# A modulation gate's matrix-vector product: column tiles of the tensor engine, or sums on the vector engine between z's projections

## The chip, the core and the metric

The kernel runs on one core of one Trainium2 chip. The core has a tensor engine (PE) with its weight loads (PEld), a vector engine (DVE), a scalar engine (ACT), a GpSimd engine (POOL), and a sync engine (SP), which here issues nearly all DMA loads from one in-order queue. The metric is the device time of one execution in microseconds (us). Runs of this kernel differ by about 0.3%.

## What is computed

One decoder layer over 512 tokens of width 1024, in fp32. The input is normalised and modulated by a vector `c`; it is projected to the queries, keys and values of two head groups and to two gates `z_a`, `z_b`; group A does sliding-window attention with sinks, group B sparse attention with three branches (compressed, selected, window); each group's output is multiplied by SiLU(z); a last projection is scaled by the modulation's `gate` and added to the input.

```python
def hybrid_layer(x, c, w_ada, b_ada, ...):
    mod = jax.nn.silu(c) @ w_ada + b_ada
    shift, scale, gate = jnp.split(mod, 3, axis=-1)
    h = rms_norm(x, norm_gain) * (1 + scale[:, None, :]) + shift[:, None, :]
    proj = h @ w_in
    (q_a, k_a, v_a, z_a, q_b, kc, vc, ks, vs, kw, vw, z_b, g_b) = jnp.split(proj, ...)
    ...
    y = jnp.concatenate([o_a * jax.nn.silu(z_a), o_b * jax.nn.silu(z_b)], axis=-1)
    return x + gate[:, None, :] * (y @ w_out)
```

The case is about `gate` alone: 1024 values, each a sum over 1024 rows of the last third of `w_ada`, weighted by silu(c). `sc_col` holds silu(c) as 8 columns of 128 (one for each block of 128 rows), and `scz` the same columns padded to 32 wide with zeros for use as weights of a narrow matmul.

## The kernel before

The work runs in stages. The first (to about 57 us) computes shift and scale, normalises, and projects group A's q, k and v. The second (to about 164 us) projects group B's keys and values and its queries while group A's attention runs. The third (to about 270 us) projects z while group B's attention runs. The last is the output projection.

Attention runs in *slots* (one head of each of two groups of keys, one block of 128 queries). `run()` takes a slot through four steps: scores on PE; the row maximum on DVE, the exponential on ACT and the scaling by the reciprocal sum on DVE; transposes on PE, which ACT copies; and the product with the values on PE. Four slots are in different steps at a time. Between the steps `stream.adv(...)` draws work from a generator: `gen1()` in stage two, `gen2()` in stage three. `gen2()` runs the eight units of z's projection, `unit_col(...)`, eight blocks each; in each block are three matmuls of 128x512. fp32 weights are used as a high and a low part: `split()` (lines 171 and 172) makes `wh` on ACT and `wl` on DVE out of a raw tile. `with_posts()` runs one step of the first generator in the list `posts` with each block of a unit; `post_z` (SiLU) is put at the front of that list after each unit.

Raw weights come in 512 KB halves through `load_next()`, which issues the next of a fixed list (`raw_order`: ..., z_a0, gate0, z_a1, gate1, z_b0, gate2, z_b1, gate3, o0 to o3) on SP. It is called when a raw tile has had its last use; the new tile takes a free buffer of the pool, and its load waits for whatever last used that buffer. Since SP works in order, a load that waits holds those behind it.

The gate is made in four slices of 256 columns. `gate_slice(q)` multiplies with 8 calls of 128x32 by 128x256 (16 matmuls, since an fp32 matmul takes two) into four column tiles of one PSUM bank, and ACT copies the bank to `gacc`. The partition sums of `gacc` follow much later, with the first unit of the output projection (`pg`). `run()` calls a slice after the values' products of each of the first four of group B's eight groups of slots. Lines after the changed function stand 3 to 6 higher in the numbering of the changed kernel (scores L878 become L884, transposes L926/L936 become L932/L942, value products L953/L959 become L959/L965, gate sums L1033 become L1036).

Of the kernel before, what the change touches and what calls it, by code (L numbers as in the profile page):

```python
# [13 lines left out]
AF = mybir.ActivationFunctionType  # L14
OP = mybir.AluOpType
# [66 lines left out]
def hybrid_layer_kernel(ctx, tc, A, out):  # L82
    nc = tc.nc
    PE, DVE, ACT, POOL, SP = nc.tensor, nc.vector, nc.scalar, nc.gpsimd, nc.sync
# [9 lines left out]
    def T2(dt, name):  # L94
        return t2.tile([128, S], dt, name=name, tag="t2")
# [31 lines left out]
    gacc = con.tile([128, D], F32, name="gacc")  # L127
# [3 lines left out]
    sc_col = con.tile([128, 8], F32, name="sc_col")  # L131
# [13 lines left out]
    raws, pieces, pending = {}, {}, list(raw_order)  # L145

    def load_next():
        if pending:
            g, h = pending.pop(0)
            n = A["w_" + g].shape[3]  # L150
            t = rawp.tile([128, 4, GW], F32, name="raw")
            SP.dma_start(t[:, :, 0:n], A["w_" + g][h])
            raws[g, h] = t[:, :, 0:n]
# [53 lines left out]
    scz = con.tile([128, 8, 32], F32, name="scz")  # L207
# [92 lines left out]
    with in_order(tc) as begun:  # L300
# [29 lines left out]
        for k in range(8):  # L330
# [7 lines left out]
            if k % 4 == 3:  # L338
# [3 lines left out]
                for tb in range(NB):  # L342
                    PE.matmul(pr[:, tb:tb + 1], sacc[:, tb * 128:(tb + 1) * 128], ones, start=k == 3 and tb == 0,
                              stop=k == 7 and tb == NB - 1, skip_group_check=True)
# [113 lines left out]
    def W2(name, shape=(128, 512)):  # L458
        return mp.tile(list(shape), F32, name=name, tag="w2", bufs=5)
# [6 lines left out]
    def PJ():  # L466
        n_pj[0] += 1
        return (ps_px if n_pj[0] % 3 == 0 else ps_pj).tile([128, 512], F32, name="pj")
# [14 lines left out]
    def unit_col(g, ch, bank, src=(hh, hl)):  # L483

        for k in range(8):
            split_to(g, 2 * ch + k // 4, AHEAD)
            wh, wl = (x[:, k % 4, :] for x in pieces[g, 2 * ch + k // 4])
            for m, (w, h) in enumerate(((wh, src[0][k]), (wh, src[1][k]), (wl, src[0][k]))):
                PE.matmul(bank, w, h, start=k == 0 and m == 0, stop=k == 7 and m == 2)  # L489
            yield 0.65  # L490
# [3 lines left out]
    @contextmanager  # L494
    def block():

        with in_order(tc, chain, PE.engine) as last:
            yield
        chain.update(last)
# [209 lines left out]

    def gate_slice(q):  # L710

        pm = PJ()[:, 0:256]
        for h in range(2):
            for c in range(4):
                PE.matmul(pm[32 * c:32 * c + 32, :], scz[:, 4 * h + c, :], raws[f"gate{q}", h][:, c], start=h == 0,  # L715
                          stop=h == 1, skip_group_check=True)
            load_next()
        ACT.activation(gacc[:, 256 * q:256 * q + 256], pm, AF.Copy)

    posts = []  # L720

    def with_posts(gen):

        for cost in gen:
            if posts:
                c = next(posts[0], None)
                if c is None:
                    posts.pop(0)
                else:
                    cost += c  # L730
            yield cost

    def flush_posts():
        while posts:
            yield from posts.pop(0)
# [62 lines left out]
    def post_z(n, b):  # L798
        t = W2("zth")
        ACT.activation(t, b, AF.Tanh, scale=0.5)  # L800
        z = W2("sza") if n < 4 else T2(F32, "szb")
        DVE.scalar_tensor_tensor(z, t, 1.0, b, op0=OP.add, op1=OP.mult)
        yield 0.0
        if n < 4:
            make_y(n, o_a[n], z)
        else:
            sz[n - 4] = z
# [3 lines left out]
    def make_y(c, o, z):  # L811

        yf = W2("yf")
        DVE.scalar_tensor_tensor(yf, o, 0.5, z, op0=OP.mult, op1=OP.mult)
        yh[c], yl[c] = T2(F32R, f"yh{c}"), T2(F32R, f"yl{c}")
        ACT.activation(yh[c], yf, AF.Copy)
        DVE.tensor_tensor(yl[c], yf, yh[c].bitcast(F32), op=OP.subtract)

    def gen2():
        posts.append(cmp_attn())  # L820
        for n in range(8):
            b = PJ()
            yield from with_posts(unit_col(f"z_{'ab'[n // 4]}{n % 4 // 2}", n % 2, b))
            posts.insert(0, post_z(n, b))
        yield from flush_posts()


# [9 lines left out]
    def load_bias_b(r):  # L837
        for g in range(2):
            t = mp.tile([128, 512], F32, name="bias", bufs=4)
            src = line_d[1, 4 * g + r:4 * g + r + 1, :]  # L840
            SP.dma_start(t, bass.AP(tensor=src.tensor, offset=src.offset, ap=[[1, 128], [1, 512]]))
            bias["b", r, g] = t
# [51 lines left out]
    def slot_scale(sl):  # L894
        kind, r, br, i = sl["id"]
        P, dn, w = sl["P"], sl["dn"], sl["w"]
        gates = grev.rearrange("p i (g r c) -> p i g r c", g=2, c=3)[:, i, :, r]
        if br == 3:
            rr = sm.tile([128, 2, 2], F32, name="rr2", bufs=2)
            DVE.reciprocal(rr, dn)  # L900
            for g in range(2):
                for b in range(2):
                    v = P[:, g, 128 * b:128 * b + 128]
                    DVE.tensor_scalar(v, v, rr[:, g, b:b + 1], gates[:, g, 1 + b:2 + b], op0=OP.mult, op1=OP.mult)
            return
        rr = sm.tile([128, 2], F32, name="rr", bufs=4)
        DVE.reciprocal(rr, dn)
        for g in range(2):
            v = P[:, g, 0:w]
            if kind == "b":  # L910
                DVE.tensor_scalar(v, v, rr[:, g:g + 1], gates[:, g, br:br + 1], op0=OP.mult, op1=OP.mult)  # L911
            elif g:
                ACT.activation(v, v, AF.Copy, scale=rr[:, g:g + 1])
            else:
                DVE.tensor_scalar(v, v, rr[:, g:g + 1], None, op0=OP.mult)

    def slot_trans(sl):
        kind, r, br, i = sl["id"]
        P, w = sl["P"], sl["w"]
        nb = w // 128  # L920
        if nb <= 2:
            T = T2(F32, "ptT").rearrange("p (g b q) -> p g b q", g=2, b=2)
            pt = PT()
            for g in range(2):
                for b in range(nb):
                    PE.transpose(pt[:, (nb * g + b) * 128:(nb * g + b + 1) * 128], P[:, g, b * 128:(b + 1) * 128], ident)  # L926
            ACT.copy(T[:, :, 0:nb, :], rev(pt[:, 0:2 * nb * 128].rearrange("p (g b q) -> p g b q", g=2, b=nb)))  # L927
            sl["T"] = [T[:, g] for g in range(2)]
        else:
            sl["T"] = []  # L930
            for g in range(2):
                T = T2(F32, "ptT").rearrange("p (b q) -> p b q", b=4)  # L932
                sl["T"].append(T)
                pt = PT()
                for b in range(nb):
                    PE.transpose(pt[:, b * 128:(b + 1) * 128], P[:, g, b * 128:(b + 1) * 128], ident)  # L936
                ACT.copy(T[:, 0:nb, :], rev(pt[:, 0:nb * 128].rearrange("p (b q) -> p b q", b=nb)))
# [29 lines left out]
                o_a["b", r] = T2(F32, f"ob{r}")  # L967
                ACT.activation(o_a["b", r], o, AF.Copy)

    def run(slots, stream, more):  # L970

        n = len(slots)
        group = []
        for t in range(n + 3):
            per = PER_A if t < 16 else PER_B[t - 16 >= PER_B[2]]
            if t < n:
                kind, r, br, i = slots[t]["id"]
                if kind == "a" and i == 0 and r >= 2:
                    load_bias_b(r - 2)
            if 0 <= t - 2 < n:  # L980
                with block():
                    slot_trans(slots[t - 2])
            if 0 <= t - 1 < n:
                slot_scale(slots[t - 1])
            if t < n:
                with block():
                    slot_scores(slots[t])
            stream.adv(per / 2)
            if 0 <= t - 3 < n:
                group.append(slots[t - 3])  # L990
                kind, r, br, i = slots[t - 3]["id"]
                if i == NB - 1:
                    with block():
                        for sl in group:
                            slot_pv(sl)
                        if more and kind == "b":
                            more.pop(0)()
                    group = []
                    if kind == "b" and br == 2 and r + 2 < 4:
                        load_bias_b(r + 2)  # L1000
            stream.adv(per / 2)
# [7 lines left out]
    stream = Stream(gen12())  # L1009
# [3 lines left out]
    for r in range(3, 0, -1):  # L1013
        posts.insert(0, prep_q_a(r))
    run([{"id": ("a", r, 0, i)} for r in range(4) for i in range(NB)]
        + [{"id": ("b", r, *bi)} for r in range(4) for bi in [(3, 0)] + [(br, i) for br in (1, 2) for i in range(1, NB)]],
        stream, [lambda q=q: gate_slice(q) for q in range(4)])
    stream.drain()
    for r in range(4):
        if 4 + r not in yh:  # L1020
# [3 lines left out]
    gate = con.tile([128, 8], F32, name="gate")  # L1024
    pg = PJ()

    for n in range(8):
        xr = mp.tile([128, S], F32, name="xr", tag="qc", bufs=2)
        ACT.dma_start(xr, A["xT"][n])
        b = PJ()  # L1030
# [5 lines left out]
        f = W2("fin")  # L1036
# [72 lines left out]
```

## Time and profile before

| | us |
|---|---|
| median of three runs | 331.12 (330.75 to 331.83) |
| the profiled execution | 331.1 |
| its span, first to last instruction | 328.9 |
| PE busy | 320.3 |
| weight loads busy | 262.9 |
| DVE busy | 225.5 |
| ACT busy | 197.8 |

In the rows of a profile the first number is the start (timeline, chain) or the share; `x16` counts instructions; what stands in brackets or behind the last bar is the idle time of that engine just ahead, with what ended it. Tile names go without their buffer numbers.

### The profile page before, as it was taken

The numbers are of one execution on the slowest core, as the hardware profiler recorded it, in microseconds if no ns is written. First come the engines' busy times: TensorE is split into PE (matmuls) and PEld (weight loads), VectorE is DVE, ScalarE is ACT, GpSimd is POOL, SyncE is SP. The second block draws the span as 40 slices with busy tenths as digits, with TensorE's granted clock in tenths as the row PEclk, the third lists the DMA queues.
The fourth block names the chain that finished last, engine by engine and source line by source line (L and its number), as shares of the span: only waits on it lengthen the run. The fifth ranks groups of instructions, "written<-read, shape, count | busy, mean of one in ns | idle before, by whom it ended". The sixth has DMA issues, their size and how long they took to land.

```text
span 328.9 us, 6232 instructions
## 1 busy us (share of the span) xinstructions
PE 320.3 (97%) x2304; PEld 262.9 (80%) x2304; DVE 225.5 (69%) x661; ACT 197.8 (60%) x478; POOL 4.6 (1%) x22
## 2 busy tenths in 40 slices
PE   8999999999999899999999999999999999999995
PEld 3577888879999779999977778678788788788884
DVE  3557697999896248787899799686576784543320
ACT  5674645656887355994967758878487586421200
POOL 1000000000000000000000000000000000000000
PEclk9999999999999999999999999999999999999999
DMA  7999966600050883122042260535240022152321
GB/s 222 388 408 410 397 222 182 247 0 3 3 159 0 276 282 117 32 65 67 32 129 81 78 229 3 190 123 200 66 128 2 0 67 64 34 161 69 123 64 64
DMA packets 31062, 44.27 MB, mean 135 GB/s; under 512 B 1767, under 2 KB 23399, under 8 KB 31033
## 3 DMA queue, kind: packets, MB, share of 16 engines
q1 hardware_dynamic: 29880, 41.79, 37.4%
q10 hardware_dynamic: 1152, 2.10, 2.2%
q8 instruction: 18, 0.29, 0.4%
q14 instruction: 12, 0.09, 0.1%
HBM read 41.74 MB, written 2.14 MB: 133 GB/s over the span
## 4 chain that ended last, share of the span: by engine, by line
PE 83%; DVE 7%; ACT 6%; DMA 2%; issue 1%; SPq 0%; ACTq 0%; DVEq 0%
PE pj L489 31%; PE sq L296 7%; PE pj L479 7%; PE s L878 6%; PE po L953 6%; PE pt L936 4%; PE skv L297 3%; PE skv L322 3%; PE pt L926 3%; PE s L614 2%; DMA raw<-in_w_cmp 2%; ACT pa L890 2%; PE pj L229 2%; PE po L959 1%; PE pj L715 1%
## 5 line engine op out<-in xcount | busy, mean ns | idle before, releaser
L171 ACT ACTIVATE wh<-raw 128x512 fp32r<-128x512 f32 (+1 forms) x52 | 31.4, 631 | 38.0 <-PE pj L489 31.5
L172 DVE TENSOR_TENSOR wl<-raw,wh 128x512 fp32r<-128x512 f32 (+1 forms) x52 | 35.1, 692 | 12.2 <-ACT wh L171 10.6
L479 PE MATMUL pj<-wl,hh 128*128 128x256 f32 (+1 forms) x128 | 36.9, 288 | 0.8 <-DVE wl L172 0.8
L479 PE MATMUL pj<-wh,hh 128*128 128x256 f32 (+1 forms) x128 | 37.1, 291 | 0.1
L479 PE MATMUL pj<-wh,hl 128*128 128x256 f32 (+1 forms) x128 | 37.0, 289 | 0.0
L890 ACT ACTIVATE pp<-pp,nm 128x256 f32<-128x256 f32 (+2 forms) x48 | 29.3, 612 | 10.9 <-DVE nm L883 10.8
L489 PE MATMUL pj<-hh,wh 128*128 128x512 f32 x80 | 32.4, 406 | 0.0
L489 PE MATMUL pj<-hl,wh 128*128 128x512 f32 x80 | 31.8, 397 | 0.0
L489 PE MATMUL pj<-hh,wl 128*128 128x512 f32 x80 | 31.6, 395 | 0.0
L883 DVE CUSTOM_DVE_ANT_0 pp<-s,bias 128x256 f32<-128x256 f32 (+2 forms) x48 | 25.4, 551 | 8.6 <-PE s L878 8.4
L489 PE MATMUL pj<-yh,wh 128*128 128x512 f32 x64 | 25.5, 399 | 0.0
L489 PE MATMUL pj<-yh,wl 128*128 128x512 f32 x64 | 25.3, 395 | 0.0
L489 PE MATMUL pj<-yl,wh 128*128 128x512 f32 x64 | 25.2, 394 | 0.0
L479 PEld LDWEIGHTS pj<-wl,hh 128*128 128x128 f32 x128 | 24.1, 188 | 1.3 <-DVE wl L172 1.0
L479 PEld LDWEIGHTS pj<-wh,hh 128*128 128x128 f32 x128 | 24.0, 188 | 1.0 <-issue 0.5
L479 PEld LDWEIGHTS pj<-wh,hl 128*128 128x128 f32 x128 | 24.1, 188 | 0.6 <-issue 0.6
L878 PE MATMUL s<-kTb,qs 128*128 128x256 f32 (+2 forms) x96 | 23.2, 359 | 0.0
L1037 DVE SCALAR_TENSOR_TENSOR fin<-pj,gate,xr 128x512 f32<-128x512 f32 x8 | 6.0, 751 | 24.6 <-PE pj L489 24.6
L911 DVE TENSOR_SCALAR pp<-pp,rr,grev 128x256 f32<-128x256 f32 (+2 forms) x48 | 21.0, 476 | 0.5
L883 DVE CUSTOM_DVE_ANT_0 pa<-s,bias,nsink 128x256 f32<-128x256 f32 (+1 forms) x32 | 14.2, 448 | 10.1 <-PE pj L479 4.4
L927 ACT COPY ptT<-pt 128x512 f32<-128x512 f32 (+1 forms) x28 | 15.3, 547 | 7.2 <-PE pt L926 7.0
L489 PEld LDWEIGHTS pj<-hh,wh 128*128 128x128 f32 x80 | 15.0, 188 | 4.7 <-issue 2.1
(241 smaller groups left out, 724.9 us busy)
## 6 DMA issues: line engine op xcount, KB each, us to landing
ada_ring<-in_w_ada_ss SPq DMA_DIRECT2D x16, 512.0 KB, 7.2
raw<-in_w_cmp SPq DMA_DIRECT2D x8, 512.0 KB, 6.7
raw<-in_w_gate SPq DMA_DIRECT2D x8, 512.0 KB, 3.8
raw<-in_w_o SPq DMA_DIRECT2D x8, 512.0 KB, 3.9
wst_ring<-in_w_qkv_a SPq DMA_DIRECT2D x8, 384.0 KB, 8.1
xTp<-in_xT SPq DMA_DIRECT2D x8, 256.0 KB, 5.4
bias<-line_d SPq DMA_DIRECT2D x8, 256.0 KB, 4.1
raw<-in_w_q_b SPq DMA_DIRECT2D x4, 512.0 KB
```

The costliest lines, as they stand in the source:

```text
L171: ACT.activation(wh, src, AF.Copy)
L172: DVE.tensor_tensor(wl, src, wh.bitcast(F32), op=OP.subtract)
L296: PE.matmul(pj_q[tb], lt, w[:, 0:512], start=f, stop=l, skip_group_check=True)
L479: PE.matmul(bank[:, t * n:(t + 1) * n], h[:, tb * 128:(tb + 1) * 128], w[:, k % 2, :], start=k == 0 and m == 0, stop=k == 7 and m == 2)
L489: PE.matmul(bank, w, h, start=k == 0 and m == 0, stop=k == 7 and m == 2)
L878: PE.matmul(ps, qs[h][:, 128 * i:128 * i + 128], k[:, hl_, lo:lo + w], start=hl_ == 0, stop=hl_ == 1)
L883: DVE.tensor_tensor_reduce(out=P[:, g, 0:w], in0=ps, in1=bt, scale=1.0, scalar=init, op0=OP.add, op1=OP.min, accum_out=nm[:, g:g + 1])
L890: ACT.activation(P[:, g, 0:e], P[:, g, 0:e], AF.Exp, bias=nm[:, g:g + 1], scale=-1.0, accum_out=dn[:, g:g + 1])
L911: DVE.tensor_scalar(v, v, rr[:, g:g + 1], gates[:, g, br:br + 1], op0=OP.mult, op1=OP.mult)
L927: ACT.copy(T[:, :, 0:nb, :], rev(pt[:, 0:2 * nb * 128].rearrange("p (g b q) -> p g b q", g=2, b=nb)))
L936: PE.transpose(pt[:, b * 128:(b + 1) * 128], P[:, g, b * 128:(b + 1) * 128], ident)
L953: PE.matmul(o[64 * g:64 * g + 64, 128 * i:128 * i + 128], vb[:, 64 * g:64 * g + 64], sl["T"][g][:, b, :], start=first_of and b == 0, stop= ...
```

## The change

`gate_slice(q)` becomes a generator of eight DVE operations: one `tensor_scalar` and seven `scalar_tensor_tensor`, each multiplying a 128x256 block of the raw tile by a column of `sc_col` and adding to the same 256 columns of `gacc`. After each second operation it yields, so that two of them go with one block of a z unit. `gen2()` appends a slice to `posts` after every second unit of z. The matmuls, the PSUM bank and the ACT copy go, and `run()` has no list of slices any more. `load_next()` stays, one after each half.

```diff
     def gate_slice(q):
-        pm = PJ()[:, 0:256]
+        acc = gacc[:, 256 * q:256 * q + 256]
         for h in range(2):
             for c in range(4):
-                PE.matmul(pm[32 * c:32 * c + 32, :], scz[:, 4 * h + c, :], raws[f"gate{q}", h][:, c], start=h == 0,
-                          stop=h == 1, skip_group_check=True)
+                w, by = raws[f"gate{q}", h][:, c], sc_col[:, 4 * h + c:4 * h + c + 1]
+                if h == 0 and c == 0:
+                    tc.keep_in_program_order(DVE.tensor_scalar(acc, w, by, None, op0=OP.mult))
+                else:
+                    DVE.scalar_tensor_tensor(acc, w, by, acc, op0=OP.mult, op1=OP.add)
+                if c % 2:
+                    yield 0.0
             load_next()
-        ACT.activation(gacc[:, 256 * q:256 * q + 256], pm, AF.Copy)
...
             yield from with_posts(unit_col(f"z_{'ab'[n // 4]}{n % 4 // 2}", n % 2, b))
             posts.insert(0, post_z(n, b))
+            if n % 2:
+                posts.append(gate_slice(n // 2))
...
-    def run(slots, stream, more):
+    def run(slots, stream):
...
-                        if more and kind == "b":
-                            more.pop(0)()
...
-        stream, [lambda q=q: gate_slice(q) for q in range(4)])
+        stream)
```

On PE, before, at the third slice (just behind the value products of a group of slots; `pj` is a unit's bank, `pt` the transposes of the probabilities `pp`, `s` scores):

```order
L953 MATMUL po_2923<-ptT_2846,vs_100 64x128
L715 MATMUL pj_2946<-raw_2555,scz_116 32x256 x4
L715 MATMUL pj_2946<-raw_2570,scz_116 32x256 x4
L489 MATMUL pj_2876<-hh2_79,wh_2558 128x512
L489 MATMUL pj_2876<-hl2_87,wh_2558 128x512
L489 MATMUL pj_2876<-hh2_79,wl_2559 128x512
L936 MATMUL pt_2964<-first_72,pp_2857 128x128 x3
L936 MATMUL pt_2970<-first_72,pp_2857 128x128 x3
```

The same place after:

```order
L959 MATMUL po_2893<-ptT_2798,vs_100 64x128
L489 MATMUL pj_2852<-hh2_79,wl_2823 128x512
L489 MATMUL pj_2852<-hh3_80,wh_2822 128x512
L489 MATMUL pj_2852<-hl3_88,wh_2822 128x512
L489 MATMUL pj_2852<-hh3_80,wl_2823 128x512
L489 MATMUL pj_2852<-hh4_81,wh_2826 128x512
L489 MATMUL pj_2852<-hl4_89,wh_2826 128x512
L942 MATMUL pt_2922<-first_72,pp_2809 128x128 x3
L942 MATMUL pt_2928<-first_72,pp_2809 128x128 x3
```

The slices are gone; up to these transposes PE has done five matmuls more of z's than before.

On DVE, before, ahead of the scaling (L911) whose result those transposes take (`pp`; the ISA rows are the row maximum of scores, `wl` a split, `sza` and `yf` SiLU and the gated output):

```order
L172 TENSOR_TENSOR wl_2621<-raw_2549,wh_2620 128x512
L907 RECIPROCAL rr_2897<-dn_2859 128x2
L883 ISA pp_2901,nm_2902<-s_2904,bias_1730 128x512
L883 ISA nm_2902 128x1
L802 SCALAR_TENSOR_TENSOR sza_2888<-zth_2886,pj_2749 128x512
L911 TENSOR_SCALAR pp_2857<-pp_2857,rr_2897,grev_103 128x384 x2
```

The same place after, with the last two sums of the first slice:

```order
L719 SCALAR_TENSOR_TENSOR gacc_93<-raw_1457,sc_col_97,gacc_93 128x256
L889 ISA pp_2871,nm_2872<-s_2874,bias_1730 128x512
L889 ISA nm_2872 128x1
L719 SCALAR_TENSOR_TENSOR gacc_93<-raw_1457,sc_col_97,gacc_93 128x256
L913 RECIPROCAL rr_2867<-dn_2811 128x2
L889 ISA pp_2871,nm_2872<-s_2878,bias_1732 128x512
L889 ISA nm_2872 128x1
L172 TENSOR_TENSOR wl_2827<-raw_2787,wh_2826 128x512
L172 TENSOR_TENSOR wl_2831<-raw_2305,wh_2830 128x512
L172 TENSOR_TENSOR wl_2837<-raw_2787,wh_2836 128x512
L917 TENSOR_SCALAR pp_2809<-pp_2809,rr_2867,grev_103 128x384 x2
```

Two sums of the slice and three splits in a row now stand ahead of the scaling; the splits were spread out before.

On SP's queue, before, from z_b0's second half on:

```order
L152 DMA raw_2549<-in_w_z_b0 128x4x256
L152 DMA raw_2555<-in_w_gate2 128x4x256
L152 DMA raw_2570<-in_w_gate2 128x4x256
L152 DMA raw_2624<-in_w_z_b1 128x4x256
L152 DMA raw_2736<-in_w_z_b1 128x4x256
L152 DMA raw_2742<-in_w_gate3 128x4x256
L841 DMA bias_3122<-line_d_94 128x512
```

And after:

```order
L152 DMA raw_2787<-in_w_z_b0 128x4x256
L847 DMA bias_3086<-line_d_94 128x512
L152 DMA raw_2834<-in_w_gate2 128x4x256
L152 DMA raw_2840<-in_w_gate2 128x4x256
L152 DMA raw_2850<-in_w_z_b1 128x4x256
L847 DMA bias_3088<-line_d_94 128x512
L152 DMA raw_2962<-in_w_z_b1 128x4x256
L152 DMA raw_2978<-in_w_gate3 128x4x256
```

A bias load has moved ahead of gate2, and the waits are others. `raw_2834` (gate2's first half) now waits for the first slice's last sum, `raw_2840` for the split `wl_2831`, and `raw_2850` (z_b1's first half) stands behind them; `raw_2978` waits for the second slice's last sum. Before, gate2's halves and z_b1's waited for matmuls of slices and for a split. Since the pool gives buffers by what is free, some earlier raw tiles get other buffers too, with the rows themselves as they were: the two loads of q_b0 wait for early splits on ACT instead of a split and a matmul of cmp0's first quarter, and cmp1's fourth quarter waits for a split of q_b0 (`wl_1091`), which it did not before.

## The prediction

> **What bounds the kernel now.** I read the page first: the span, the busy time of each engine, and the chain that ended last by engine.
>
> ```profile
> span 328.9 us, 6232 instructions
> PE 320.3 (97%) x2304; PEld 262.9 (80%) x2304; DVE 225.5 (69%) x661; ACT 197.8 (60%) x478; POOL 4.6 (1%) x22
> PE 83%; DVE 7%; ACT 6%; DMA 2%; issue 1%; SPq 0%; ACTq 0%; DVEq 0%
> ```
>
> The profiled execution took 331.1 us, so 2.2 us lie around its span; the median of the runs shown is 331.12 us, and no correction is needed between the two. TensorE (PE) is busy for 97% and carries 83% of the chain; the rest of the chain is mostly VectorE (DVE) and ScalarE (ACT). What counts is the stage in which the change lies, so I read the busy time by stretches (columns: PE, weight loads, DVE, ACT, POOL, clock, DMA share, GB/s).
>
> ```profile
> 188.00:208.00 20.00, 19.99 (x182) 15.58 (x182) 18.19 (x58) 13.41 (x36) 0.00 (x0) 1.00 0.41 132
> 208.00:224.00 16.00, 16.00 (x142) 12.78 (x131) 11.66 (x36) 12.18 (x32) 0.00 (x0) 1.00 0.47 152
> 224.00:240.00 16.00, 16.00 (x125) 12.51 (x124) 9.31 (x34) 10.72 (x31) 0.00 (x0) 1.00 0.34 114
> 240.00:256.00 16.00, 16.00 (x122) 13.70 (x121) 11.57 (x43) 11.75 (x33) 0.00 (x0) 1.00 0.21 67
> 256.00:276.00 20.00, 20.00 (x168) 16.38 (x166) 15.71 (x47) 13.79 (x38) 0.00 (x0) 1.00 0.17 54
> ```
>
> PE has no gap from 188 to 276 us and its clock is full. DVE is busy 48.25 us of the 68 us from 208 on, so it idles for 19.75 us there. Work taken off PE shortens this stage one for one, as long as DVE and ACT still deliver the probabilities in time.
>
> **What is removed.** The views are the chain, which has all four gate slices, and the groups by line.
>
> ```profile
> 191.43 1.00 PE pj L715 x16
> 207.47 1.00 PE pj L715 x16
> 220.76 1.00 PE pj L715 x16
> 233.58 1.00 PE pj L715 x16
> L715 PE MATMUL pj<-raw,scz 128*32 128x256 f32 x64 | 4.3, 385 | 0.0
> L718 ACT ACTIVATE gacc<-pj 128x256 f32<-128x256 f32 x4 | 1.5, 385 | 1.8 <-PE pj L715 1.8
> ```
>
> Each slice holds the chain for 1.00 us: 4 x 1.00 = 4.0 us go from PE, all on the path. The four ACT copies (1.5 us) lie beside PE; nobody waits for them before the end, so I count nothing.
>
> **What is added.** Four times one multiply and seven multiply-adds on DVE, 128x256 each. The nearest rows are the same two operations on the same shapes in the first stage.
>
> ```profile
> L220 DVE SCALAR_TENSOR_TENSOR macc<-ada_ring,sc_col,macc 128x256 f32<-128x256 f32 x18 | 7.8, 478 | 0.0
> L218 DVE TENSOR_SCALAR macc<-ada_ring,sc_col 128x256 f32<-128x256 f32 x6 | 1.8, 348 | 0.7 <-ACT hh L286 0.7
> 29.64 1.27 DVE L220 SCALAR_TENSOR_TENSOR macc<-ada_ring,sc_col,macc 128x256 f32<-128x256 f32 x3
> ```
>
> Three in a row took 1.27 us, so each starts 0.40 us behind the last ((1.27 - 0.478) / 2). Those alternate between two accumulators; the new ones add to one, and a dependent one may take its whole 0.478. So the change adds between 28 x 0.40 + 4 x 0.30 = 12.4 us and 28 x 0.478 + 4 x 0.348 = 14.8 us; I take 13, nearer the lower end, since most stand between other operations. That is less than the 19.75 us of idle time, but it is worth nothing on average: what counts is each place where PE waits for DVE. The Trainium skill (VectorE: DVE Perf Modes, "The DRAIN you can't avoid") says that the next DVE operation does not begin before the pipe of the last is empty; by it the sum would be the 14.8 us. The 1.27 us row overlaps the operations by 0.08 us each, so the rule does not hold for independent ones, and no row here has dependent ones of this kind.
>
> **Place one: the first slice, up to the transposes at 222.49.** Before, DVE starts the scores of a slot at 209.57 and ends the scaling of another at 219.16 (218.30 + 0.86); PE transposes the latter only at 222.49.
>
> ```profile
> 209.57 0.69 DVE L883 CUSTOM_DVE_ANT_0 pp<-s,bias 128x512 f32<-128x512 f32 x1 [1.80 <-PE s L878]
> 213.65 0.17 DVE L907 RECIPROCAL rr<-dn 128x2 f32<-128x2 f32 x1 [0.32 <-ACT pp L890]
> 216.43 0.69 DVE L172 TENSOR_TENSOR wl<-raw,wh 128x512 fp32r<-128x512 f32 x1 [0.88 <-ACT wh L171]
> 218.30 0.86 DVE L911 TENSOR_SCALAR pp<-pp,rr,grev 128x384 f32<-128x384 f32 x2
> 222.49 0.82 PE L936 MATMUL pt<-first,pp 128*128 128x128 f32 x6
> 252.27 0.39 PE L489 MATMUL pj<-hh,wh 128*128 128x512 f32 x1
> 252.50 0.39 PE L489 MATMUL pj<-hl,wh 128*128 128x512 f32 x1
> ```
>
> After, the same stretch of DVE holds all eight operations of the first slice and two splits (wl) more. Of the 9.6 us before, 1.2 were idle (0.32 and 0.88 in the rows); 8.4 + 0.3 + 7 x 0.40 + 2 x 0.6 = 12.7, and 13.0 if a quarter of the idle time stays. It begins 2.0 us earlier (two slices gone), at 207.6, and ends at 220.6. PE reaches those transposes 3.0 us earlier, with five more of z's matmuls ahead of them (0.23 us each, the two last rows): 222.49 - 3.0 + 1.16 = 220.65. The two meet to within tenths; at 0.478 per operation PE would wait 0.6 us. The other slices, placed in the same way, leave margins from 0.1 to over 3 us; the last one lies between the last slots' scores, where PE has o0's matmuls for cover. For the four I take 0.6 us of new PE waits for DVE, with 0 as the low end. The high end is one whole slice uncovered, 7 x 0.478 + 0.348 = 3.7 us.
>
> **Place two: the loads on SP.** A raw tile is released later when DVE reads it, so SP's in-order queue waits for other things. Before, it waited for PE at these loads.
>
> ```profile
> SPq L152 <- PE pj L715: 19.5, 4, 11.8
> raw<-in_w_gate SPq DMA_DIRECT2D x8, 512.0 KB, 3.8
> 223.59 0.29 DVE L854 CUSTOM_DVE_ANT_0 pp<-s,bias 128x128 f32<-128x128 f32 x1 [1.12 <-PE s L852]
> 224.97 0.69 DVE L172 TENSOR_TENSOR wl<-raw,wh 128x512 fp32r<-128x512 f32 x1 [0.45 <-ACT wh L171]
> 251.08 0.69 DVE L172 TENSOR_TENSOR wl<-raw,wh 128x512 fp32r<-128x512 f32 x1 [0.68 <-ACT wh L171]
> 256.33 0.70 DVE L172 TENSOR_TENSOR wl<-raw,wh 128x512 fp32r<-128x512 f32 x1
> ```
>
> Now gate2's halves wait for the first slice's last sum and for a split, and z_b1's first half is queued behind both. By the sum above that split ends 0.8 us before those 220.6, at 219.8; plus a landing of 3.8 to 5 us (with two other loads beside it), z_b1 is there at 223.6 to 224.8. Its first split follows the next slot's first operations, which stand at 223.59 to 224.97 now; they move by -3.0 + 1.16, to 221.8 to 223.1, and the split now stands behind that slot's four exponentials on ACT, say 1.1 us more: 224.2. So it is 0 to 0.6 us late; I take 0.4. Behind it on DVE stands that slot's scaling, for which PE then waits. o0's second half waits for the third slice's fourth sum, just ahead of the split at 251.08: issued at about 247.3, landed by 251.2, and its split, at 256.33 now, is due at 252.3. The other loads of o wait for later sums and splits and are wanted later still. I count nothing for these; what hides them is z's matmuls.
>
> **Place three: earlier, without an edit there.** The allocator gives the raw tiles other buffers, so two early loads change their waits.
>
> ```profile
> 106.62 0.51 SPq L152
> 107.18 5.93 DMA raw<-in_w_cmp
> 113.15 0.71 PE L614 MATMUL s<-raw,pp 128*64 128x256 f32 x2 [1.30 <-DMA raw<-in_w_cmp]
> 114.89 0.69 DVE L172 TENSOR_TENSOR wl<-raw,wh 128x512 fp32r<-128x512 f32 x1 [2.19 <-ACT wh L171]
> 120.10 2.00 PE L614 MATMUL s<-raw,pp 128*64 128x256 f32 x14
> raw<-in_w_cmp SPq DMA_DIRECT2D x8, 512.0 KB, 6.7
> ```
>
> Before, cmp0's third quarter was issued at 107.18, behind a q_b load whose buffer came free at 106.6, and PE waited 1.30 us for it. After, those loads wait for splits of about 90 us: the 1.30 us go. But cmp1's fourth quarter now waits for a split that cannot come before about 114.2 (it ends at 115.58 now, less 1.3); with 3.8 to 6.7 us it lands at 118.0 to 120.9, and PE wants it at 120.10 - 1.30 = 118.8. So 0 to 2.1 us come back; I take 0.6, at the usual 5 us. Place three: -1.3 + 0.6 = -0.7 us (ends -1.3 and +0.8).
>
> **Sum.** 331.1 - 4.0 - 0.7 + 0.6 + 0.4 = 327.4 us. All favourable ends give 331.1 - 4.0 - 1.3 = 325.8; all unfavourable 331.1 - 4.0 + 0.8 + 3.7 + 0.6 = 332.2.
>
> **Rivals.**
>
> (a) DVE becomes what PE waits for in the group b slots, and the gain is eaten. For it: the waits between the engines there are already short and many, so a late scaling goes on to ACT and back.
>
> ```profile
> ACT pp L890 <- DVE nm L883: 10.8, 17, 1.1
> DVE pp L883 <- PE s L878: 8.0, 5, 3.6
> DVE rr L907 <- ACT pp L890: 6.6, 12, 1.0
> ```
>
> Against it: none of these waits ends in PE, whose gaps are nil. It needs 4.0 + 0.7 us of stalls, more than a whole slice of DVE's time: 331.1 us, no change.
>
> (b) Slower: z_b1's first half comes late. It lands 6 us later than reckoned if the split in front of it on SP is held by DVE, as SP was held up to 11.8 us by PE before. Then ACT's split, DVE's split and the scaling behind it hold PE: 327.4 + 6 = 333.4 us. It decides from 4.7 us late on. Against it: the split is one of three in a row that PE itself needs at about that time.
>
> (c) PE's freed time is not on the end. PE's weight loads are busy for only 80%, 12.78 of 16 us in the stretch from 208 on, and the slices could lie where these catch up: then removing the slices frees nothing, 331.1 us. The Trainium skill (Perfetto Trace Analysis, "Identifying the Most-Contended Engine") says that matmul busy time is no good measure for TensorE and that busy weight loads are. Against it here: the chain steps from one z matmul to the next each 0.23 us (rows above), and waits for nothing.
>
> (d) No stall at all: 325.8 us; it is the low end of the forecast, not a case apart.
>
> **How the numbers follow.** The forecast's mechanism (4.0 us kept but for up to 3 us of stalls) has 0.72; (a) 0.12, (b) 0.10, (c) 0.06. Changes under 0.3%, 1.0 us, cannot be told from none here, so faster means under 330.1 and slower over 332.1. Faster: 0.72. Same: (c) and two thirds of (a), 0.14. Slower: (b) and the rest of (a), 0.14. The range runs from 325.6, just under the favourable end, to 331.6, which takes in most of (a) and (c) and leaves out (b).
>
> **What would show it.** In the trace after: no rows of the slices on PE, and PE's busy time down by about 4 us; DVE's up by 13 to 15 us; the 1.30 us wait at cmp gone, with a wait of under 2 us at its fourth quarter; transposes (L942) or z matmuls with waits on DVE of under 1 us each. I am wrong if PE's waits after 188 us come to over 3 us, or if the wait for z_b1's load shows on ACT with more than 2 us.

## The result, and the profile after

| | before | after |
|---|---|---|
| median of the runs, us | 331.48 (330.75 to 332.10) | 325.97 (325.57 to 326.38) |
| ratio to before | | 0.983 (95% interval 0.981 to 0.985) |
| profiled execution and its span, us | 331.1, 328.9 | 325.85, 323.8 |

The kernel became 5.5 us faster; 3.7 us were forecast. The head of the page of the changed kernel, its busy times and its chain by engine:

```profile
span 323.8 us, 6133 instructions
PE 316.6 (98%) x2240; PEld 261.3 (81%) x2240; DVE 236.0 (73%) x693; ACT 196.3 (61%) x474; POOL 4.5 (1%) x22
PE 86%; ACT 6%; DVE 6%; issue 1%; ACTq 0%; DVEq 0%
```

PE's busy time fell by 3.7 us (320.3 to 316.6) and its 64 slice matmuls are gone. DVE's rose by 10.5 us (225.5 to 236.0). DMA no longer has a share of the chain. The same stretches of the third stage as before the change (columns as there):

```profile
188.00:208.00 20.00, 20.00 (x161) 16.57 (x157) 17.59 (x59) 13.53 (x36) 0.00 (x0) 1.00 0.23 74
208.00:224.00 16.00, 16.00 (x122) 13.36 (x121) 15.92 (x53) 11.84 (x34) 0.00 (x0) 1.00 0.42 129
224.00:240.00 16.00, 15.96 (x112) 12.56 (x110) 14.16 (x44) 12.32 (x34) 0.00 (x0) 1.00 0.41 136
240.00:256.00 16.00, 16.00 (x146) 13.69 (x144) 14.06 (x51) 11.60 (x32) 0.00 (x0) 1.00 0.22 67
256.00:276.00 20.00, 20.00 (x160) 16.51 (x158) 15.29 (x44) 12.74 (x31) 0.00 (x0) 1.00 0.33 106
```

PE still has no gap, though DVE (third figure) now works 15.92 of 16 us from 208 to 224, where it worked 11.66 before. So the time of the slices went, and no wait took its place.

Where the 5.1 us of the span went is read by cutting both executions at the same three instructions: cmp's first matmul, z's first matmul, and the last `fin`, which ends the output projection. Timeline rows of before, then of after:

```profile
104.56 2.01 PE L614 MATMUL s<-raw,pp 128*64 128x256 f32 x16
163.85 0.40 PE L489 MATMUL pj<-hh,wh 128*128 128x512 f32 x1
325.33 0.75 DVE L1037 SCALAR_TENSOR_TENSOR fin<-pj,gate,xr 128x512 f32<-128x512 f32 x1 [4.82 <-PE pj L489]
```

```profile
105.17 2.01 PE L614 MATMUL s<-raw,pp 128*64 128x256 f32 x16
163.13 0.40 PE L489 MATMUL pj<-hh,wh 128*128 128x512 f32 x1
320.23 0.75 DVE L1040 SCALAR_TENSOR_TENSOR fin<-pj,gate,xr 128x512 f32<-128x512 f32 x1 [4.84 <-PE pj L489]
```

- Up to cmp: 104.56 to 105.17, so 0.61 us longer. The edit does not reach there; over this study's profiles this instant lies between 104.56 and 105.49, and before's is the earliest of all.
- The *middle*, cmp to z: 59.29 to 57.96, so 1.33 us shorter.
- The *last part*, z to the end: 161.48 to 157.10, so 4.38 us shorter. This is where the slices were.

The sum, +0.61 - 1.33 - 4.38 = -5.1 us, is the whole difference of the spans. Middle and last part are the measure for the experiments below, since what happens up to cmp is the same work in all of them.

### The profile page after: what moved, and what is told of

It reads as the page before. It is cut to its first block, busy times and chain, and to the rows that moved or that the text cites. A ratio compares the mean times of both kernels' runs of the same rounds, so it can differ in the third digit from the quotient of the medians.

```text
span 323.8 us, 6133 instructions
## 1 busy us (share of the span) xinstructions
PE 316.6 (98%) x2240; PEld 261.3 (81%) x2240; DVE 236.0 (73%) x693; ACT 196.3 (61%) x474; POOL 4.5 (1%) x22
## 4 chain that ended last, share of the span: by engine, by line
PE 86%; ACT 6%; DVE 6%; issue 1%; ACTq 0%; DVEq 0%
PE pj L489 31%; PE pj L479 8%; PE sq L296 7%; PE s L884 7%; PE po L959 7%; PE pt L942 4%; PE skv L297 4%; PE pt L932 3%; PE skv L322 3%; PE s L614 3%; ACT pa L896 2%; PE pj L229 2%; PE pt L536 1%; PE po L965 1%; DVE wl L172 1%
## 5 line engine op out<-in xcount | busy, mean ns | idle before, releaser
L943 ACT COPY ptT<-pt 128x384 f32<-128x384 f32 (+1 forms) x32 | 15.7, 528 | 5.1 <-PE pt L942 4.8
```

## The experiments

The theory: the last part is shorter because the slices' matmuls were on the path and the DVE sums are hidden; the middle is shorter because an early load no longer makes PE wait, which the allocation of buffers brought and not the edit as such. The rivals: that the new place (with z's blocks) is what pays, whichever engine does the work; that the sums cost something, hidden behind a larger gain; that removed matmul time does not count in full.

In the table, middle and last part are read from each profile at the same three instructions. One of the six executions with 16 more sums took 611.94 us, for a reason that the record doesn't show; the ratio leaves it out.

| kernel | median, us | ratio to before (95%) | middle | last part |
|---|---|---|---|---|
| before | 331.5 | | 59.29 | 161.48 |
| after | 325.97 | 0.983 (0.981 to 0.985) | 57.96 | 157.10 |
| slices on PE, in after's place | 331.85 | 1.0015 (0.9992 to 1.0038) | 59.17 | 161.88 |
| sums on DVE, in before's place | 325.59 | 0.982 (0.980 to 0.984) | 57.57 | 157.57 |
| before, other list of loads | 330.16 | 0.996 (0.994 to 0.997) | 57.45 | 161.42 |
| after, other list of loads | 325.67 | 0.982 (0.980 to 0.984) | 58.08 | 157.08 |
| the last one, sums 8 columns wide | 324.87 | 0.980 (0.979 to 0.981) | 57.26 | 156.96 |
| before, other list, slices' matmuls twice | 332.87 | 1.004 (1.003 to 1.005) | 57.84 | 164.43 |
| after, other list, 16 more sums | 329.21 | 0.992 (0.989 to 0.995) | 57.95 | 161.45 |
| after, other list, 32 more sums | 336.39 | 1.016 (1.013 to 1.019) | 58.09 | 167.11 |
| after, other list, 64 more sums | 349.83 | 1.055 (1.053 to 1.057) | 57.94 | 181.61 |
| after, a third list of loads | 325.83 | 0.982 (0.979 to 0.984) | 57.58 | 157.38 |

### The engine or the place

The slices on PE, but drawn from `posts` as in the changed kernel:

```diff
-        acc = gacc[:, 256 * q:256 * q + 256]
+        pm = PJ()[:, 0:256]
...
-                    DVE.scalar_tensor_tensor(acc, w, by, acc, op0=OP.mult, op1=OP.add)
-                if c % 2:
-                    yield 0.0
+                PE.matmul(pm[32 * c:32 * c + 32, :], scz[:, 4 * h + c, :], raws[f"gate{q}", h][:, c], start=h == 0,
+                          stop=h == 1, skip_group_check=True)
             load_next()
+        ACT.activation(gacc[:, 256 * q:256 * q + 256], pm, AF.Copy)
+        yield 0.0
```

> The slices stay on PE as column tiles with ACT's copy, but are called where the change puts the sums, as posts behind every second unit of z. The early loads here wait as in the kernel before. Theory (engine and early wait are all, the place is nothing): as before, 331.3 us within 0.5, with PE's 1.3 us wait for cmp. Rival (the other place and order of the third stage give part of the gain): under 330.3 us.

The sums on DVE, all eight of a slice in a block, called by `run()` where the slices were:

```diff
-        pm = PJ()[:, 0:256]
+        acc = gacc[:, 256 * q:256 * q + 256]
...
-                PE.matmul(pm[32 * c:32 * c + 32, :], scz[:, 4 * h + c, :], raws[f"gate{q}", h][:, c], start=h == 0,
-                          stop=h == 1, skip_group_check=True)
+                if h == 0 and c == 0:
+                    DVE.tensor_scalar(acc, w, by, None, op0=OP.mult)
+                else:
+                    DVE.scalar_tensor_tensor(acc, w, by, acc, op0=OP.mult, op1=OP.add)
             load_next()
-        ACT.activation(gacc[:, 256 * q:256 * q + 256], pm, AF.Copy)
```

> The eight sums of a slice on DVE, but all in one go at the place where the slices stood on PE before, behind the value products of a group of slots. The early loads wait as in the changed kernel. Theory (DVE has room anyway, and PE has z's matmuls for cover): as the changed kernel, 326.0 to 327.0 us. Rival (the spreading over z's blocks is what hides the sums; a slice in one go holds the scalings for 3.4 us): one to three us slower than the changed kernel, 327 to 329 us, with waits of PE's transposes for DVE's scalings.

The engine decides and the place does not. With the slices on PE in the new place nothing is gained (last part 161.88); with the sums on DVE, called at the old place, nearly everything is (157.57, 3.91 us less than before). In that kernel the sums in fact run from 131 to 228 us, partly in stage two, so that it tries an earlier place rather than exactly the old one; it is as fast as the changed kernel, and a little faster than the 326 to 327 us that were expected.

The middle, before and after (length, then the busy time of PE, weight loads, DVE, ACT):

```profile
104.56:163.85 59.29, 57.10 (x494) 52.00 (x493) 38.74 (x140) 40.90 (x115) 1.70 (x8) 1.00 0.37 121
```

```profile
105.17:163.13 57.96, 57.12 (x493) 52.07 (x493) 38.73 (x140) 40.91 (x115) 1.70 (x8) 1.00 0.30 96
```

PE does the same work in both (57.10 and 57.12 us); the 1.33 us are idle time that went, and the wait for cmp was 1.30 of it. The kernel with the slices on PE in the new place agrees. It keeps the wait of before, here in its timeline, and its middle is as long as before's:

```profile
113.76 0.71 PE L614 MATMUL s<-raw,pp 128*64 128x256 f32 x2 [1.12 <-DMA raw<-in_w_cmp]
```

The changed kernel and the one with the block of sums have no such wait and are 1.33 and 1.72 us shorter there. So the middle goes with the buffers that the early loads get, which differ from build to build.

### The early loads apart

The third quarters of cmp are listed ahead of q_b0's loads, once in the kernel before and once in the changed one:

```diff
-    raw_order += [(f"cmp{kv}", q) for q in range(2) for kv in range(2)] + [("q_b0", 0), ("q_b0", 1)]
-    raw_order += [(f"cmp{kv}", q) for q in range(2, 4) for kv in range(2)]
+    raw_order += [(f"cmp{kv}", q) for q in range(2) for kv in range(2)] + [("cmp0", 2), ("cmp1", 2)]
+    raw_order += [("q_b0", 0), ("q_b0", 1), ("cmp0", 3), ("cmp1", 3)]
```

> The kernel before with one edit: in the list of raw loads q_b0's two halves stand behind the third quarters of cmp0 and cmp1 instead of ahead of them, so that these no longer queue behind a load whose buffer comes free at 106.6 us. Theory (the 1.30 us wait of PE for cmp was lost time on the path, and the change removed it by giving other buffers): about 1.3 us faster than before, 330.0 us, with no wait of PE for cmp. Rival (the early gain is swallowed later in the second stage, and all 5 us came from the third): no change, 331.3 us.

> The changed kernel with the same edit of the list of loads. Theory: its wait for cmp is gone already, so nothing changes, 326.0 us, and the difference to the kernel before with that edit is the four slices, 4.0 us, less what the sums cost. Rival (the change's own gain in the third stage is 5 us): the difference is 5 us or more.

The list alone gives before 1.4 us (330.16 against 331.58 in the same series), all of it in the middle (-1.84, with 0.46 us more up to cmp); its last part stays as it was (-0.06). So the middle's gain is to be had without touching the gate. It is not the same gain in each piece: with this list the wait at cmp is still 0.4 us, and PE's busy time in the middle is 56.25 us instead of 57.10, with PE's matmuls in another order there; what shortened it was not followed up.

In the changed kernel the list brings a wait back, at cmp's fourth quarter:

```profile
119.09 2.00 PE L614 MATMUL s<-raw,pp 128*64 128x256 f32 x14 [1.07 <-DMA raw<-in_w_cmp]
```

PE's busy time in its middle is 56.24 us, so the wait uses up what the list saves, and the middle stays as it was (58.08 against 57.96). The expectation that nothing would change came true by this balance, and not because there was nothing left to wait for. Less this wait, which is 0.3 to 1.1 us long, the middle is 57.0 to 57.1 us in all seven kernels with this list.

With the same list on both sides the change itself is worth 330.16 - 325.67 = 4.5 us, and 161.42 - 157.08 = 4.34 us in the last part. That is more than the slices' 4.0 us. The timeline of before shows why:

```profile
191.04 0.40 PE L489 MATMUL pj<-hh,wh 128*128 128x512 f32 x1
191.36 1.07 PE L715 MATMUL pj<-raw,scz 128*32 128x256 f32 x16
192.36 0.51 PE L489 MATMUL pj<-hl,wh 128*128 128x512 f32 x1
192.71 0.39 PE L489 MATMUL pj<-hh,wl 128*128 128x512 f32 x1
```

From the z matmul ahead of the slice to its first one it is 0.32 us, and from the first z matmul behind it to the next 0.35 us, where z matmuls follow each other in 0.23 us. A slice so costs its 1.00 us and up to 0.2 us of slower steps around it; the third and fourth slices are left with 0.34 us as well. Over all four slices the last part shows 0.4 us beyond their own rows, so not every edge costs as much.

### The slices' price, from the other side

The eight matmul calls of a slice are done twice (unmarked lines differ in their indentation alone, and the call is shortened):

```diff
+        for t in range(2):
             for h in range(2):
                 for c in range(4):
                     PE.matmul(pm[32 * c:32 * c + 32, :], scz[:, 4 * h + c, :], raws[f"gate{q}", h][:, c], ...)
-            load_next()
+        load_next()
+        load_next()
```

> The kernel before with the same order of loads, and each slice's 16 matmuls on PE done twice in a row (the second starts the sum anew, so the output is as before). It prices a slice without the step into and out of it. Theory (a slice holds PE 1.00 us, and the step from z's matmuls to it and back costs 0.1 us more): +4.0 us over the kernel before with that order, 334.2 us, and 4.0 us in the third stage, where taking the slices out gave 4.4. Rival (a slice costs 1.1 us all through): +4.4 us in the third stage.

The last part grew by 164.43 - 161.42 = 3.0 us, less than the 4.0 us expected and the 4.4 us of the rival. The first slice in its timeline:

```profile
190.73 1.93 PE L716 MATMUL pj<-raw,scz 128*32 128x256 f32 x32
192.60 0.50 PE L489 MATMUL pj<-hl,wh 128*128 128x512 f32 x1
192.93 0.39 PE L489 MATMUL pj<-hh,wl 128*128 128x512 f32 x1
```

32 matmuls take 1.87 us to the next start, 16 took 1.00: the second 16 cost 0.87 us, and they add no step in or out. Four times 0.87 are 3.5 us; the other 0.5 us are missing in PE's other rows of the last part, and why remains open. Taken together: removing the four slices is worth 4.4 us and not 4.0, because the change of form goes with them.

### Are the sums hidden, and by how much

The sums do the same instructions on 8 of the 256 columns (the rest of `gacc` is zero):

```diff
-        acc = gacc[:, 256 * q:256 * q + 256]
+        acc = gacc[:, 256 * q:256 * q + 8]
...
-                w, by = raws[f"gate{q}", h][:, c], sc_col[:, 4 * h + c:4 * h + c + 1]
+                w, by = raws[f"gate{q}", h][:, c, 0:8], sc_col[:, 4 * h + c:4 * h + c + 1]
```

> The changed kernel with q_b0 behind cmp's third quarters, and with sums over only 8 of each slice's 256 columns (the rest of the gate stays zero, so the output lacks most of it); the number of operations and their places stay. DVE's work falls by some 9 us. Theory (the sums are wholly hidden): as the changed kernel with that order, 325.7 us within 0.4, and the same third stage. Rival (PE does wait for the sums, spread over many places too small for the table of waits): 0.5 to 1.5 us faster, 324.2 to 325.2 us.

Now the other way: a repeated sum per pair of blocks (16 more), per block (32 more), or two repeats per block (64 more). The diff of the 32:

```diff
                     DVE.scalar_tensor_tensor(acc, w, by, acc, op0=OP.mult, op1=OP.add)
+                DVE.scalar_tensor_tensor(acc, w, by, acc, op0=OP.mult, op1=OP.add)
                 if c % 2:
                     yield 0.0
```

> The same order of loads, and every sum of the gate done twice (so the gate's products are twice what they should be, less the first block's extra): 32 operations more on DVE, about 13 us. From 188 to 284 us DVE idles for 14.8 us of 96 in the changed kernel. Theory (hidden as long as DVE has idle time near each place): the margin is nearly used up, 326.5 to 329 us, with the first waits of PE for DVE. Rival (DVE's idle time can be used wholly): 325.7 us.

> As the last, with every sum three times: about 26 us more on DVE against 14.8 us of idle time. Theory: DVE becomes the bound of the third stage and the excess of 11 us appears in the time, less what moves outside that stretch: 333 to 338 us. Rival (PE's other work lets DVE lag into the output projection, where it idles): under 331 us.

> The changed kernel with q_b0 behind cmp's third quarters and every second sum of a slice done twice: 16 operations, about 6.5 us, more on DVE (the gate's values are wrong by those blocks). Doubling all sums added 13 us to DVE and 10.0 us to the third stage, so DVE's idle time there can hardly be used. Theory one (the changed kernel stands at an edge; each further us of DVE costs nearly a us): about 5 us slower, 330 to 331 us. Theory two (there is room for several us, and the last ones cost most): under 327.5 us.

Busy time from 188 to 284 us, in this order: the changed kernel, the narrow sums, 16 more sums, 32 more sums (PE, weight loads, DVE, ACT).

```profile
188.00:284.00 96.00, 95.96 (x741) 78.63 (x737) 81.41 (x254) 65.02 (x169) 0.00 (x0) 1.00 0.30 96
```

```profile
188.00:284.00 96.00, 96.00 (x727) 79.08 (x724) 74.59 (x253) 63.78 (x169) 0.00 (x0) 1.00 0.31 98
```

```profile
188.00:284.00 96.00, 93.99 (x725) 76.57 (x723) 83.55 (x264) 63.06 (x165) 0.00 (x0) 1.00 0.31 98
```

```profile
188.00:284.00 96.00, 91.64 (x688) 73.06 (x684) 89.10 (x279) 62.96 (x166) 0.00 (x0) 1.00 0.29 94
```

Downwards next to nothing is left to gain: the narrow sums take some 6.6 us off DVE (81.20, the same window of the kernel they are cut from, to 74.59) and the last part is 0.12 us shorter. The kernel's time, 324.87 us, lies in the range of the rival, but its 0.8 us lie in the middle, where its wait for cmp is 0.3 us and not 1.1, and no sum runs there. So this part of the sums' time costs about 0.1 us. The narrow operations still take DVE some time of their own, which was not removed; that this costs nothing either rests on the table of PE's waits, which has no row behind 188 us in the changed kernel.

Upwards it is another matter. 16 more sums, each 0.40 us to the next start, are 6.4 us of DVE (its busy time rose by 6.3 us); the last part grew by 161.45 - 157.08 = 4.37 us. 32 more (12.1 us of busy time) cost 10.03 us, 64 more (25.4 us) 24.5 us. All three missed what was expected: 329.21 us lies between the two theories, and 336.39 and 349.83 us are beyond theory and rival alike. The longest of PE's waits from 160 us on, with 16 more sums and then with 32 (line waited for, total, times, longest); in the changed kernel this table is empty:

```profile
PE pj L489 <- ACT yh L822: 1.0, 1, 1.0
PE pt L934 <- DVE pp L912: 0.9, 1, 0.9
PE pj L1038 <- DVE gacc L721: 0.8, 1, 0.8
```

```profile
PE pt L943 <- DVE pp L918: 2.6, 4, 1.9
PE pj L489 <- ACT yh L821: 1.5, 1, 1.5
```

PE now waits for the scalings (`pp`), for the gated output (`yh`) whose input DVE makes, and for the last sums themselves. With 16 more sums all such waits come to 2.9 us, at full clock; the other 1.5 us of the 4.37 stand in longer rows of PE's, and were not followed up. The changed kernel has 96.00 - 81.41 = 14.6 us of idle DVE in this window, and yet two thirds of another 6.4 us land on the end. The change stands just ahead of that edge. With 32 more the granted clock also fell, to 0.93 from 276 to 292 us, and with 64 more to 0.91 over the whole window, so their 10.03 and 24.5 us are not all waits.

### A version that takes both

The narrow kernel's 0.8 us in the middle suggested a third order of the early loads, with the full sums:

```diff
+    raw_order += [(f"cmp{kv}", q) for q in range(2) for kv in range(2)]
+    raw_order += [('q_b0', 0), ('cmp0', 2), ('cmp1', 2), ('q_b0', 1), ('cmp0', 3), ('cmp1', 3)]
```

> The changed kernel with cmp's third quarters between the two halves of q_b0 in the list of loads; all sums as in the change. In this build the early loads get buffers that let cmp's third quarters go out at about 94 us, q_b0's second half and cmp0's fourth quarter right behind, and cmp1's fourth quarter at about 113 us. Theory (the kernel with narrow sums was 0.8 us faster through its early loads, not through its sums): 324.9 us within 0.3, with no wait of PE for cmp and a third stage as in the changed kernel. Rival (it was the sums): 325.7 us.

It gave 325.83 us and not the 324.9 expected: a wait of 0.6 us at cmp is left, and it can't be told from the changed kernel. No version tried with full sums is clearly faster than the changed kernel; the best three are 325.59, 325.67 and 325.83 us against its 325.97.

## Why the prediction was right, point by point

**The slices (-4.0 us): right in kind, too small.** They were on the path, as the chain had it: -4.38 us in the last part, -4.34 with the same list of loads on both sides. The term was mis-sized because only the slices' own rows were counted and not the slower step into and out of them (0.32 and 0.35 us instead of 0.23).

**The sums (13 us of DVE).** Rows of the groups after, and two of the timeline:

```profile
L719 DVE SCALAR_TENSOR_TENSOR gacc<-raw,sc_col,gacc 128x256 f32<-128x256 f32 x28 | 13.4, 477 | 0.0
L717 DVE TENSOR_SCALAR gacc<-raw,sc_col 128x256 f32<-128x256 f32 x4 | 1.4, 346 | 0.0
212.43 0.48 DVE L719 SCALAR_TENSOR_TENSOR gacc<-raw,sc_col,gacc 128x256 f32<-128x256 f32 x1
212.83 0.41 DVE L917 TENSOR_SCALAR pp<-pp,rr,grev 128x256 f32<-128x256 f32 x1
```

The instructions last 0.477 us, but the next one starts after 0.40 us, the lower of the two prices. DVE's busy time rose by 10.5 us and not by 13 to 15: that step was too high, also against 28 x 0.40 + 4 x 0.26 = 12.2 us from these starts, and the rest was not followed up. The worry over dependent sums was right only where two stand directly behind each other on one accumulator, which is rare in the changed kernel. In the kernel with the sums in a block they do so oftener, and the second begins 1.00 - 0.48 = 0.52 us behind the first; at 248.48 us two sums of the changed kernel take the same 1.00 us:

```profile
152.43 1.00 DVE L719 SCALAR_TENSOR_TENSOR gacc<-raw,sc_col,gacc 128x256 f32<-128x256 f32 x2
```

The Trainium skill (VectorE: DVE Perf Modes, "The DRAIN you can't avoid"), which was quoted for the price of 14.8 us, adds there that a next operation that is not held starts earlier; the 0.40 us from the row at 212.43 to the next agrees with that clause, and the 14.8 us are not borne out.

**Place one (a meeting to within tenths).** After, DVE ends the scaling at 219.29 and PE takes it up at 219.33, without a wait in the row:

```profile
216.62 1.89 DVE L172 TENSOR_TENSOR wl<-raw,wh 128x512 fp32r<-128x512 f32 x3
218.43 0.86 DVE L917 TENSOR_SCALAR pp<-pp,rr,grev 128x384 f32<-128x384 f32 x2
219.33 0.82 PE L942 MATMUL pt<-first,pp 128*128 128x128 f32 x6
```

220.6 and 220.65 were forecast; both came 1.3 us earlier, of which 0.72 us are the earlier start of z (163.13 instead of 163.85) that this step's sum had left out. The margin of 0.04 us is as narrow as forecast. The 0.6 us taken for PE's waits did not come: the table of PE's waits after 188 us is empty, and making the sums narrow gains 0.12 us. With two terms each more than 1 us off by the same amount, that the margin came out as forecast is in part luck.

**Place two (z_b1's load, 0.4 us): the queue as reckoned, the lateness not.** The load was issued behind gate2's two (SP), at 218.58 and so 1.2 us earlier than the 219.8 of the forecast, and its first split on ACT ran at 224.31, forecast 224.2, with no wait; the second half was waited for by ACT for 0.98 us, but not by PE:

```profile
216.07 2.41 SPq L152 DMA_DIRECT2D raw<-in_w_gate  x2
218.58 0.58 SPq L152 DMA_DIRECT2D raw<-in_w_z_b  x1
224.31 0.62 ACT L171 ACTIVATE wh<-raw 128x512 fp32r<-128x512 f32 x1
227.86 1.16 ACT L171 ACTIVATE wh<-raw 128x512 fp32r<-128x512 f32 x2 [0.98 <-DMA raw<-in_w_z_b]
```

**Place three (-0.7 us): right in sign, half the size.** The 1.30 us wait went as reckoned (-1.33 us in the middle). The 0.6 us that was to come back did not: cmp1's fourth quarter was issued at 114.87, for an earliest 114.2 forecast, and PE, which wants it at 119.35, did not wait, so it landed within 4.5 us and not in the 5 us taken.

```profile
114.87 0.55 SPq L152 DMA_DIRECT2D raw<-in_w_cmp  x1
119.35 2.00 PE L614 MATMUL s<-raw,pp 128*64 128x256 f32 x14
```

**The sum.** Against the forecast gain of 3.7 us the span shows 5.1: 0.4 us more from the slices, 0.6 from place three, 1.0 from stalls that did not come, less the 0.61 us up to cmp that no step spoke of. The time lies at the lower end of the range, 0.4 us above its bound: nearly every open price came out at its favourable end (the case called (d)). So the path and the hiding on DVE were right, and three of the sizes were off; that 0.4 us too little for the slices nearly cancels against the 0.61 us of the start is luck.

**The rivals.** (a), DVE eats the gain, did not happen, but was the near one: 6.4 us more of DVE eat the whole gain of the last part (161.45 us, before's is 161.48), though not the middle's. Its own bound, 4.7 us of stalls, and the 14.6 us of idle time both fail to say that. (b), z_b1 late, is refuted by the row at 224.31. (c), PE's freed time is not on the end, is refuted by removing and by doubling: 4.4 us gone, 3.0 us come. The Trainium skill (Perfetto Trace Analysis, "Identifying the Most-Contended Engine") would judge TensorE's headroom by the arithmetic done and the weight loads, and these were busy 80% here; these runs differ, since each slice taken off or added moved the end by 0.75 us or more on the average of four.

## What to carry to other kernels

Where the bounding engine has no gap, work on it is worth its own rows and the slower steps into and out of another form of instruction beside them; look at the start of the neighbour on each side before pricing it. Work moved to a second engine is free only as far as no in-order wait of the first begins, and that is not read from its idle share: here the sums' 10.5 us brought PE no wait and the next 6.4 us cost 4.4, with 14.6 us of idle time in the window. When a change shifts the allocation of buffers, cut both traces at a few common instructions, so that what came with the allocation is not taken for the change (1.3 of 5.1 us here).

## What the runs showed of the hardware

The start of an execution moves by itself. PE's warm-up on a zero tile took 6.80 us before and 7.66 us after, on the same instructions:

```profile
1.22 6.80 PE L322 MATMUL skv<-zero 128*128 128x512 bf16 x24 [1.22 <-DVE wst_ring L304]
```

```profile
1.22 7.66 PE L322 MATMUL skv<-zero 128*128 128x512 bf16 x24 [1.22 <-DVE wst_ring L304]
```

That is the likely source of the 0.61 us up to cmp: from the end of this row to cmp's first matmul it is 96.54 us before and 96.29 us after, so the later start of cmp is all in these 24 matmuls. No run here was made to show why they took longer. The Trainium skill (TensorE: Matmul & The Clock Gate, "What's actually happening") says that the clock's window runs freely, so that the change to full speed comes up to half a microsecond earlier or later from run to run; these two rows, 0.86 us apart, lie within that spread, but the granted clock reads 1.00 in both profiles from 0 to 10 us, so no row here shows the change of clock itself.

Between z's matmuls, narrow column tiles have a price at their edges: 0.32 us into the group and 0.33 to 0.35 us out of it, against 0.23 us between z matmuls, while 16 more of them inside the group cost 0.87 us.
